# Streaming encoder step: the sampled streams' value products in one TensorE shape, with zero rows where the other half's new keys would be, and the value blocks of both halves moved next to each other

## The chip, the core and the metric

The kernel runs on one core of one Trainium2 chip. A core has TensorE (matrix products and transposes; PE in the profile, its weight loads PEld), VectorE (DVE), ScalarE (ACT), GpSimd (POOL) and SyncE (SP, which here only issues transfers). Each engine works through its own queue in order and waits on semaphores for the others. The metric is device time in microseconds of one execution. Three runs of the kernel before took 1458.16, 1460.51 and 1463.31 us; the median is 1460.51.

## The reference

One inference step of an encoder with two layers (width 1024, all in 32-bit floats), for a prompt of 512 frames and for 8 running streams of 16 new frames each (the "samples"). Layer 0 is a convolution module and a feed-forward part; then one shared set of keys and values is projected; layer 1 projects queries, attends to the shared keys, and has a feed-forward part of its own. The part that matters here is the samples' attention, per head (16 heads of 64):

```
def band_attention_sample(q, k_all, v_all, table):
    B, S, H, Dh = q.shape
    W = k_all.shape[1] - S
    bias = rel_bias_band(table, S, W + S, W)
    s = jnp.einsum("bqhd,bkhd->bhqk", q, k_all).astype(jnp.float32) * scale + bias
    p = jax.nn.softmax(s, axis=-1).astype(v_all.dtype)
    return jnp.einsum("bhqk,bkhd->bqhd", p, v_all).reshape(B, S, H * Dh)
```

Each stream's 16 queries see 512 cached keys and the 16 new ones, 528 in all. The prompt's 512 frames attend to each other in chunks of 64.

## The kernel before, in words

Frames lie along the free side, features along the 128 partitions: 640 columns, the 128 sample frames first. Large products are split into a rounded high part and a remainder and done as three products (`mm3`, lines 199 to 201; the feed-forward parts use line 439). The attention stage takes the 16 heads as 8 pairs of two heads (128 features). For a pair, a list of letters (`BO`, for the last pair `BL`, lines 67 and 68) sets the order in which the steps are written; the framework's list scheduler then orders each engine's instructions by its own timing estimate, and fills in projections of the next pair, output projections and, in the last pair, pieces of the output projection ("o" and "q" in `BL`).

The digit behind a letter is a head (a, b) or a half of the samples (s, t, n, c, d). A half is 4 streams with 16 frames and 2 heads: 4 x 32 rows = 128 partitions.

- `a` (`head_a`, line 1258 on): prompt scores of one head, bias and maximum on DVE, exponentials on ACT. `b` (`head_b`): ten transposes of them, copied out of PSUM in three pieces. `p` (`pair_c`, line 1326): the pair's value product (weights 128 rows x 64 columns), then split by ACT and DVE (lines 187 and 189).
- `s` (`samp_a`): the half's keys and values are loaded (2 x 512 KB each, line 1337, into 8 rotating buffers); four products of 512 cached keys (line 1342), one per stream, whose weights are 128 x 32 and whose outputs stand in 32 partitions each; four more for 64 columns of new keys (line 1345); the other streams' new keys get a large negative bias. DVE adds the bias and takes the maximum into a tile `Ss` (128 x 576, two rotating buffers), ACT makes the exponentials there.
- `t` (`samp_b`): the 512 cached columns are transposed in four pieces (line 1358) and copied by ACT into `PTs` (line 1368). `n` (its `rest`): the columns of the 64 new keys are transposed (line 1364) and copied by DVE (line 1365). Because the half's new values lie in rows 0 to 63 or 64 to 127 of the value tile `VT`, the transpose is 64 wide for the first half; for the second it takes 64 columns more so that the result lands in rows 64 to 127.
- `c` (`samp_c`): the half's value products, 16 over the cached keys (line 1378, weights 128 rows x 32 columns) and 4 over the new keys (line 1382, weights 64 rows x 32 columns), all into one PSUM tile. Each shows as two instructions in the profile (32 and 8 a block). DVE scales the rows into a tile `os` (line 1387).
- `d` (its `rest`): `os` is transposed (line 1391) and split into high part and remainder.

Transposes and value products go through two rotating PSUM buffers called `am`: each new user takes the one used before last, so it waits until that one has been copied out.

Of the kernel before, what the change touches and what calls it, by code (L numbers as in the profile page):

```python
# [8 lines left out]
F32 = mybir.dt.float32  # L9
F32R = mybir.dt.float32r  # L10
I32 = mybir.dt.int32
AF = mybir.ActivationFunctionType
# [3 lines left out]
P = 128  # L16
# [66 lines left out]
def tile_trunk(ctx, tc, xT, vecs, hist, w_pw1, w_pw2, w_in0, w_out0, w_os0, w_in1, w_out1, w_os1,  # L83
               w_kq, w_v, w_o, rel, kc, vc, y_out, convp_out, convs_out, k_out, v_out):
    nc = tc.nc
# [15 lines left out]
    def nm(s):  # L101
        uid[0] += 1
        return f"{s}_{uid[0]}"
# [19 lines left out]
    ident = cst.tile([P, P], F32, name="ident", tag="ident")  # L123
# [1074 lines left out]
    fill, step_end = None, [None]  # L1198
# [132 lines left out]
    def samp_a(p, u, st):  # L1331
        qb, kt = qbd[p % 2], kts[p]
        cache = []
        for src in (kc[p, u], vc[p, u].rearrange("p b k d -> p b (k d)")):
            for i in range(2):
                t = ap.tile([P, 2, 512], F32, tag="cache", name=nm("cache"), bufs=CB)
                nc.sync.dma_start(t, src[:, 2 * i:2 * i + 2, :])
                cache.append(t)
        KC, VC = cache[:2], cache[2:]
        qv = [qb[:, 4 * u + b, :, :].rearrange("p h q -> p (h q)") for b in range(4)]  # L1340
        for b in range(4):
            nc.tensor.matmul(st[32 * b:32 * b + 32, 0:512], qv[b], KC[b // 2][:, b % 2, :],
                             start=True, stop=True)
        for b in range(4):
            step_end[0] = nc.tensor.matmul(st[32 * b:32 * b + 32, 512:576], qv[b],
                                           kt[:, 64 * u:64 * u + 64], start=True, stop=True).ins
# [3 lines left out]
        addmax(S, st[:, 0:576], BS, mx[:, 0:1])  # L1350
        rs = softmax_rows(S, mx, sm, [(0, 576)])
        return S, rs, VC

    def samp_b(u, S):
        v0 = 64 * u
        tr = amt()
        for k in range(4):
            step_end[0] = nc.tensor.transpose(tr[:, k * P:(k + 1) * P],
                                              S[:, k * P:(k + 1) * P], ident).ins
        PT = ap.tile([P, 640], F32, tag="PTs", name=nm("PTs"), bufs=1)  # L1360

        def rest():
            tn = amt()
            step_end[0] = nc.tensor.transpose(tn[0:v0 + 64, 0:P], S[:, 512 - v0:576], ident).ins
            nc.vector.tensor_copy(PT[v0:v0 + 64, 512:640], tn[v0:v0 + 64, 0:P])
            return PT

        nc.scalar.activation(out=PT[:, 0:512], in_=tr, func=AF.Copy)
        return rest

    def samp_c(p, u, PT, rs, VC):
        v0 = 64 * u
        VT = vts[p // 2]
        pv = amt()
        for k in range(5):
            for b in range(4):
                if k < 4:
                    nc.tensor.matmul(pv[32 * b:32 * b + 32, 0:P],
                                     PT[:, k * P + 32 * b:k * P + 32 * b + 32],
                                     VC[b // 2][:, b % 2, k * P:(k + 1) * P], start=(k == 0), stop=False)  # L1380
                else:
                    step_end[0] = nc.tensor.matmul(
                        pv[32 * b:32 * b + 32, 0:P],
                        PT[v0:v0 + 64, 512 + 32 * b:512 + 32 * b + 32],
                        VT[v0:v0 + 64, 0, (p % 2) * P:(p % 2) * P + P], start=False, stop=True).ins
# [12 lines left out]

        return rest
# [18 lines left out]
    for p in range(NP):  # L1418
# [8 lines left out]
        for op in (BL if p == NP - 1 else BO).split():  # L1427
# [9 lines left out]
            elif op[0] == "n":  # L1437
                ps[i] = ps[i]()
            elif op[0] == "c":
                ps[i] = samp_c(p, i, ps[i], *sa[i][1:])  # L1440
            elif op[0] == "d":
                ps[i]()
            elif op[0] in "oq":
# [244 lines left out]
```

## Time and profile before

| | us |
|---|---|
| runs | 1458.16, 1460.51, 1463.31 |
| profiled execution, its span from first to last instruction | 1460.0 |
| convolution layer and first feed-forward part | 0 to about 660 |
| attention stage, first scores to last pair product | 695 to 1003 |
| second feed-forward part and final norm | 1003 to 1460 |

The execution that the profiler recorded has a span of 1460.0 us, which is the only time given for it; the median of the timed runs is 0.5 us above it. In the rows of the profile, "128*32" is the shape of the weights (rows by columns), then comes the shape of the moving side; "x32" counts merged instructions, and the time of such a row runs from the start of its first to the end of its last. "[0.20 <-issue]" is idle time of the engine ahead of the row, with what ended it; "issue" means that nothing in the profile was waited for. Since products overlap in the array, their durations are longer than the distance of their starts, and it is the starts that tell what a product costs.

### The profile page before, as it was taken

The numbers are of one execution on the slowest core, as the hardware profiler recorded it, in microseconds if no ns is written. First come the engines' busy times: TensorE is split into PE (matmuls) and PEld (weight loads), VectorE is DVE, ScalarE is ACT, GpSimd is POOL, SyncE is SP. The second block draws the span as 40 slices with busy tenths as digits, with TensorE's granted clock in tenths as the row PEclk, the third lists the DMA queues.
The fourth block names the chain that finished last, engine by engine and source line by source line (L and its number), as shares of the span: only waits on it lengthen the run. The fifth ranks groups of instructions, "written<-read, shape, count | busy, mean of one in ns | idle before, by whom it ended". The sixth has DMA issues, their size and how long they took to land. (4 is left out here: it accounts for less than half of the span.)

```text
span 1460.0 us, 28194 instructions
## 1 busy us (share of the span) xinstructions
PE 1434.0 (98%) x11022; PEld 1369.6 (94%) x11022; DVE 1138.9 (78%) x2520; ACT 757.8 (52%) x1628; POOL 297.6 (20%) x349
## 2 busy tenths in 40 slices
PE   9999999999999999999999999999999999999998
PEld 8998799999999999999987898878999999999998
DVE  6789867988888888756768668577898888888765
ACT  4666554654554554545654355443554564455453
POOL 5699120010111111013222121011011111111101
PEclk9999999999999999999999999999999999999999
DMA  7267434045444534425556554452125444444522
GB/s 243 73 180 187 126 86 146 14 135 150 131 108 118 163 92 135 116 88 193 181 163 213 173 192 162 138 200 67 44 82 143 135 113 129 137 120 109 155 66 72
DMA packets 66932, 192.56 MB, mean 132 GB/s; under 512 B 12144, under 2 KB 30320, under 8 KB 58480
## 3 DMA queue, kind: packets, MB, share of 16 engines
q1 hardware_dynamic: 52432, 160.58, 33.8%
q0 software_dynamic: 13504, 29.37, 9.9%
q8 instruction: 86, 1.41, 0.4%
q10 hardware_dynamic: 864, 0.83, 0.2%
q14 instruction: 46, 0.38, 0.1%
HBM read 179.14 MB, written 11.61 MB: 131 GB/s over the span
## 5 line engine op out<-in xcount | busy, mean ns | idle before, releaser
L439 PE MATMUL mm<-XH,whi 128*128 128x320 f32 x896 | 275.9, 310 | 2.9 <-ACT t L451 2.6
L439 PE MATMUL mm<-XH,wlo 128*128 128x320 f32 x896 | 276.1, 309 | 0.0
L439 PE MATMUL mm<-XL,whi 128*128 128x320 f32 x896 | 274.5, 309 | 0.0
L371 ACT ACTIVATE whi<-raw 128x512 fp32r<-128x512 f32 (+2 forms) x280 | 168.4, 613 | 135.2 <-PE mm L439 103.6
L199 PE MATMUL mm<-xh,whi 128*128 128x320 f32 (+2 forms) x640 | 200.2, 314 | 0.8 <-DVE h L702 0.4
L200 PE MATMUL mm<-xh,wlo 128*128 128x320 f32 (+2 forms) x640 | 198.2, 311 | 0.0
L372 DVE TENSOR_TENSOR wlo<-raw,whi 128x512 fp32r<-128x512 f32 (+2 forms) x280 | 183.9, 666 | 15.9 <-ACT whi L371 14.8
L201 PE MATMUL mm<-xl,whi 128*128 128x320 f32 (+2 forms) x640 | 195.9, 311 | 0.4 <-DVE xl L189 0.4
L439 PE MATMUL mm<-hid,whi 128*128 128x320 f32 x732 | 172.5, 311 | 5.5 <-DVE hid L372 3.1
L439 PEld LDWEIGHTS mm<-XH,whi 128*128 128x128 f32 x896 | 167.7, 188 | 4.9 <-ACT t L451 4.2
L439 PEld LDWEIGHTS mm<-XH,wlo 128*128 128x128 f32 x896 | 168.2, 188 | 0.0
L439 PEld LDWEIGHTS mm<-XL,whi 128*128 128x128 f32 x896 | 167.7, 188 | 0.0
L439 PEld LDWEIGHTS mm<-hid,whi 128*128 128x128 f32 x732 | 125.0, 188 | 8.8 <-DVE hid L372 4.2
L199 PEld LDWEIGHTS mm<-xh,whi 128*128 128x128 f32 x640 | 120.5, 188 | 4.0 <-ACT xh L187 1.5
L201 PEld LDWEIGHTS mm<-xl,whi 128*128 128x128 f32 x640 | 119.7, 188 | 1.2 <-DVE xl L189 0.8
L200 PEld LDWEIGHTS mm<-xh,wlo 128*128 128x128 f32 x640 | 120.5, 189 | 0.2
L439 PE MATMUL mm<-hid,wlo 128*128 128x320 f32 x366 | 113.0, 309 | 0.0
L439 PE MATMUL mm<-XH,slo 128*128 128x320 f32 x344 | 106.0, 308 | 0.0
L439 PE MATMUL mm<-XH,shi 128*128 128x320 f32 x344 | 105.8, 309 | 0.0
L439 PE MATMUL mm<-XL,shi 128*128 128x320 f32 x344 | 105.6, 308 | 0.0
L417 POOL DMA_DIRECT2D s<-in_w_in x38 | 22.1, 581 | 388.7 <-DVE wlo L372 151.8
L841 POOL TENSOR_TENSOR ca<-ca,cvt 128x512 f32<-128x512 f32 x60 | 91.9, 1532 | 17.8 <-ACT cvt L838 11.2
(275 smaller groups left out, 3370.8 us busy)
## 6 DMA issues: line engine op xcount, KB each, us to landing
raw<-in_w_in SPq DMA_DIRECT2D x38, 1024.0 KB
s<-in_w_in POOLq DMA_DIRECT2D x76, 256.0 KB, 4.2
raw<-in_w_os SPq DMA_DIRECT2D x24, 768.0 KB
cache<-in_ck SPq DMA_DIRECT2D x32, 512.0 KB
cache<-in_cv SPq DMA_DIRECT2D x32, 512.0 KB
raw<-in_w_pw SPq DMA_DIRECT2D x11, 1024.0 KB
s<-in_w_os POOLq DMA_DIRECT2D x48, 192.0 KB, 3.6
raw<-in_w_kq SPq DMA_DIRECT2D x8, 1024.0 KB
```

Of the source, the lines that this page charges most:

```text
L199: nc.tensor.matmul(ps, wh, xh, start=(first and i == 0), stop=False)
L200: nc.tensor.matmul(ps, wl, xh, start=False, stop=False)
L201: end = nc.tensor.matmul(ps, wh, xl, start=False, stop=(stop and i == last))
L371: put_end[1] = nc.scalar.activation(out=hi, in_=src, func=AF.Copy).ins
L372: put_end[0] = nc.vector.tensor_tensor(out=lo, in0=src, in1=hi.bitcast(F32), op=sub).ins
L417: nc.gpsimd.dma_start(s1, src[:, 2 * n:3 * n])
L439: last = nc.tensor.matmul(pt, wt, v, start=(first and k == i == 0), stop=(k == n - 1 and i == 2), skip_group_check=True)
L841: nc.gpsimd.tensor_tensor(out=acc, in0=acc, in1=pr, op=ALU.add)
```

## The change

Four things change, all in the attention stage.

1. The four products over the new keys take 128 rows of weights as the others do. The probabilities of the other half's 64 rows are zero: for the first half the transpose takes 128 columns, the last 64 of which are zeros (a score tile `Sn` of 640 columns, filled with zeros there once), and the copy `PM` takes all 128 rows; for the second half a tile `PN`, with rows 0 to 63 set to zero once, takes rows 64 to 127.
2. `Ss` has one buffer (second half), `Sn` is the first half's. `PTs` is 512 wide with two buffers.
3. The row-scaled output goes into the first 128 columns of the score tile in place of `os`.
4. The order of the steps: both halves are transposed before the pair's product, and `c0 c1` and `d0 d1` are neighbours (in the last pair, all ahead of `p0`).

```diff
-BO = "a0 s0 a1 s1 b0 b1 t0 n0 p0 c0 d0 t1 n1 c1 d1"
-BL = "a0 o2 s0 a1 o2 s1 q2 t0 q2 n0 b0 q2 b1 q2 c0 q2 d0 t1 q2 n1 o2 c1 o2 d1 p0 o2"
+BO = "a0 s0 a1 s1 b0 b1 t0 n0 t1 n1 p0 c0 c1 d0 d1"
+BL = "a0 o2 s0 a1 o2 s1 q2 t0 q2 n0 b0 q2 t1 q2 b1 n1 q2 c0 c1 q2 d0 o2 d1 o2 p0 o2"
...
+    Sn = ap.tile([P, 640], F32, name="Sn", tag="Sn")
+    nc.gpsimd.memset(Sn[:, 576:640], 0.0)
+    PN = ap.tile([P, P], F32, name="PN", tag="PN")
+    nc.gpsimd.memset(PN[0:64, :], 0.0)
...
-        S = ap.tile([P, 576], F32, tag="Ss", name=nm("Ss"), bufs=2)
+        S = ap.tile([P, 576], F32, tag="Ss", name=nm("Ss"), bufs=1) if u else Sn
...
-        PT = ap.tile([P, 640], F32, tag="PTs", name=nm("PTs"), bufs=1)
+        PT = ap.tile([P, 512], F32, tag="PTs", name=nm("PTs"), bufs=2)
...
-            step_end[0] = nc.tensor.transpose(tn[0:v0 + 64, 0:P], S[:, 512 - v0:576], ident).ins
-            nc.vector.tensor_copy(PT[v0:v0 + 64, 512:640], tn[v0:v0 + 64, 0:P])
-            return PT
+            step_end[0] = nc.tensor.transpose(tn[:, 0:P], S[:, 512 - v0:640 - v0], ident).ins
+            pn = PN if u else ap.tile([P, P], F32, tag="PM", name=nm("PM"), bufs=1)
+            nc.vector.tensor_copy(pn[v0:, :], tn[v0:, 0:P])
+            return PT, pn
...
-                if k < 4:
-                    nc.tensor.matmul(pv[32 * b:32 * b + 32, 0:P],
-                                     PT[:, k * P + 32 * b:k * P + 32 * b + 32],
-                                     VC[b // 2][:, b % 2, k * P:(k + 1) * P], start=(k == 0), stop=False)
-                else:
-                    step_end[0] = nc.tensor.matmul(
-                        pv[32 * b:32 * b + 32, 0:P],
-                        PT[v0:v0 + 64, 512 + 32 * b:512 + 32 * b + 32],
-                        VT[v0:v0 + 64, 0, (p % 2) * P:(p % 2) * P + P], start=False, stop=True).ins
-        os_ = ap.tile([P, P], F32, tag="os", name=nm("os"), bufs=1)
+                c = slice(k * P + 32 * b, k * P + 32 * b + 32)
+                step_end[0] = nc.tensor.matmul(
+                    pv[32 * b:32 * b + 32, 0:P], PT[:, c] if k < 4 else pn[:, 32 * b:32 * b + 32],
+                    VC[b // 2][:, b % 2, k * P:(k + 1) * P] if k < 4
+                    else VT[:, 0, (p % 2) * P:(p % 2) * P + P], start=k == 0, stop=k == 4).ins
+        os_ = S[:, 0:P]
```

The scheduler makes a new order of it on every engine, from the first pair's transposes to the first products of the second feed-forward part. Three places on TensorE follow. Lines of the changed kernel are shifted: 1309 is 1313 now, 1326 is 1330, 1358 is 1362, 1364 is 1368, and 1378 and 1382 are both 1384. The shape behind the names is that of the output.

TensorE, seventh pair, the end of the first half's value block, before (cache: the values; vt: the new ones; KK, KL, QQ: the next pair's split scores):

```order
L1378 MATMUL am_11256<-cache_11117,PTs_11240 32x128 x2
L1378 MATMUL am_11256<-cache_11119,PTs_11240 32x128 x2
L1382 MATMUL am_11256<-vt_10921,PTs_11240 32x128 x4
L1285 MATMUL w_1351_11494<-KK_11496,QQ_11498 128x512
L1286 MATMUL w_1351_11494<-KL_11497,QQ_11498 128x512
```

The same place in the changed kernel:

```order
L1384 MATMUL am_11258<-cache_11109,PTs_11231 32x128 x2
L1384 MATMUL am_11258<-cache_11111,PTs_11231 32x128 x2
L1384 MATMUL am_11258<-vt_10913,PM_11235 32x128 x4
L1384 MATMUL am_11280<-cache_11171,PTs_11242 32x128 x2
L1384 MATMUL am_11280<-cache_11173,PTs_11242 32x128 x2
```

The new keys' products are of the line and shape of the others, and the second half's block follows at once. This is so in the fifth, seventh and eighth pairs; in the first four and the sixth other products stand between the two blocks.

TensorE, seventh pair, the transposes ahead of the pair's product, before (S: prompt probabilities; Ss: a half's; PT with vt: the pair's product):

```order
L201 MATMUL mm_11442<-xl_7448,whi_11325 128x384
L1309 MATMUL am_11231<-ident,S_11138 128x128 x2
L1358 MATMUL am_11235<-ident,Ss_11129 128x128 x4
L1364 MATMUL am_11242<-ident,Ss_11129 64x128
L1326 MATMUL am_11245<-PT_11201,vt_10921 64x512
```

and now:

```order
L201 MATMUL mm_11432<-xl_7448,whi_11315 128x384
L1313 MATMUL am_11216<-ident,S_11129 128x128 x4
L1313 MATMUL am_11222<-ident,S_11129 128x128 x2
L1362 MATMUL am_11226<-ident,Sn 128x128 x4
L1368 MATMUL am_11233<-ident,Sn 128x128
L1362 MATMUL am_11237<-ident,Ss_11183 128x128 x4
L1368 MATMUL am_11244<-ident,Ss_11183 128x128
L1330 MATMUL am_11247<-PT_11192,vt_10913 64x512
```

Six users of the two `am` buffers stand in a row ahead of the pair's product, where there were three; in the fifth pair, too, the second half's transposes stand right ahead of it.

TensorE, eighth pair, the first half's remainder and the first head's transposes, before:

```order
L1364 MATMUL am_11678<-ident,Ss_11567 64x128
L1309 MATMUL am_11682<-ident,S_11491 128x128 x4
L1309 MATMUL am_11688<-ident,S_11491 128x128 x4
L1309 MATMUL am_11694<-ident,S_11491 128x128 x2
L199 MATMUL mm_11698<-ohi_9955,whi_11530 128x320
```

and now:

```order
L1368 MATMUL am_11667<-ident,Sn 128x128
L199 MATMUL mm_11659<-ohi_9951,whi_11520 128x320
L200 MATMUL mm_11659<-ohi_9951,wlo_11521 128x320
L201 MATMUL mm_11659<-olo_9952,whi_11520 128x320
L199 MATMUL mm_11659<-ohi_10499,whi_11520 128x320
L200 MATMUL mm_11659<-ohi_10499,wlo_11521 128x320
L201 MATMUL mm_11659<-olo_10500,whi_11520 128x320
L1313 MATMUL am_11672<-ident,S_11481 128x128 x4
L1313 MATMUL am_11678<-ident,S_11481 128x128 x4
```

Six products of the output projection stand between them now.

More of the change, by code (lines that the diff above doesn't have):

```diff
@@ L1359, in samp_b, with samp_c @@
                                               S[:, k * P:(k + 1) * P], ident).ins
-        PT = ap.tile([P, 640], F32, tag="PTs", name=nm("PTs"), bufs=1)
+        PT = ap.tile([P, 512], F32, tag="PTs", name=nm("PTs"), bufs=2)
         def rest():
             tn = amt()
-            step_end[0] = nc.tensor.transpose(tn[0:v0 + 64, 0:P], S[:, 512 - v0:576], ident).ins
-            nc.vector.tensor_copy(PT[v0:v0 + 64, 512:640], tn[v0:v0 + 64, 0:P])
-            return PT
-        nc.scalar.activation(out=PT[:, 0:512], in_=tr, func=AF.Copy)
+            step_end[0] = nc.tensor.transpose(tn[:, 0:P], S[:, 512 - v0:640 - v0], ident).ins
+            pn = PN if u else ap.tile([P, P], F32, tag="PM", name=nm("PM"), bufs=1)
+            nc.vector.tensor_copy(pn[v0:, :], tn[v0:, 0:P])
+            return PT, pn
+        nc.scalar.activation(out=PT, in_=tr, func=AF.Copy)
         return rest
-    def samp_c(p, u, PT, rs, VC):
+    def samp_c(p, u, PTs, S, rs, VC):
         v0 = 64 * u
+        PT, pn = PTs
         VT = vts[p // 2]
@@ L1439, in tile_trunk @@
             elif op[0] == "c":
-                ps[i] = samp_c(p, i, ps[i], *sa[i][1:])
+                ps[i] = samp_c(p, i, ps[i], *sa[i])
             elif op[0] == "d":
```

2 lines of the change are left out of this document (1 added, 1 removed).

## The prediction

> **What bounds the kernel now.** I read the page first (shares by engine, then the chain that ended last), then the busy time of the attention stage alone, then TensorE's rows around one value block.
>
> ```profile
> span 1460.0 us, 28194 instructions
> PE 1434.0 (98%) x11022; PEld 1369.6 (94%) x11022; DVE 1138.9 (78%) x2520; ACT 757.8 (52%) x1628; POOL 297.6 (20%) x349
> PEclk9999999999999999999999999999999999999999
> PE 27%; DVE 2%; DMA 1%; ACT 0%; issue 0%; DVEq 0%
> ```
>
> TensorE is busy for 98% of the span at full clock, and it is the only engine with a real share of the chain. The attention stage, where all of the change lies, is no exception:
>
> ```profile
> 695.00:1003.00 308.00, 303.25 (x2742) 263.23 (x2742) 212.53 (x636) 150.77 (x404) 55.79 (x93) 1.00 0.51 169
> 960.00:1003.00 43.00, 40.18 (x402) 31.32 (x401) 29.24 (x82) 16.95 (x42) 4.61 (x9) 1.00 0.25 89
> ```
>
> The columns are length, then PE, PEld, DVE, ACT and POOL busy. PE is busy for 303 of 308 us, DVE for 213, so a microsecond taken from TensorE's own sequence here is a microsecond of the span, unless a wait takes its place. More than half of the idle time (2.8 of 4.8 us) lies in the last 43 us, where projections no longer fill the gaps. A busy PE still hides something: each product is booked for 0.27 us or more while the next starts 0.03 to 0.23 us later, so short gaps do not show as idle. They show in the starts, and in the weight loads' idle time:
>
> ```profile
> 730.26 0.81 PEld L1378 LDWEIGHTS am<-cache,PTs 128*32 128x32 f32 x32 [0.17 <-issue]
> 730.26 1.08 PE L1378 MATMUL am<-cache,PTs 128*32 128x128 f32 x32
> 731.27 0.15 PEld L1382 LDWEIGHTS am<-vt,PTs 64*32 64x32 f32 x8 [0.20 <-issue]
> 731.27 0.42 PE L1382 MATMUL am<-vt,PTs 64*32 64x128 f32 x8
> 731.62 0.19 PEld L1285 LDWEIGHTS w<-KK,QQ 128*128 128x128 f32 x1 [0.20 <-issue]
> PEld am L1382 <- issue: 3.0, 15, 0.2
> ```
>
> "128*32" is the weights' shape, rows by columns. The last row is from the waits of the stage: the first weight load of the 64*32 products stood idle for 0.2 us in 15 of 16 blocks, with nothing that the profile names to wait for, 3.0 us in all. The same pause stands wherever the shape changes, and not where it stays.
>
> **The change, term by term.**
>
> *The pause before the new keys' products (removed).* 32 products from 730.26 take 1.08 us, the last one itself 0.27, so they start every (1.08 - 0.27)/31 = 0.026 us and the last starts at 731.07. The 64*32 products start at 731.27: 0.20 after it, in place of 0.026. With all products in 128*32 the step is an ordinary one: 16 blocks x 0.174 = -2.8 us.
>
> *The products themselves (dearer).* Eight 64*32 products take (0.42 - 0.28)/7 = 0.020 us each, eight in 128*32 would take 0.026: 7 x 0.006 x 16 = +0.7 us. The weight loads say the same: 8 in 0.15 us there, 32 in 0.81 here.
>
> *Shape changes next to the blocks.* Over the whole order of the eight pairs I count the points where neighbouring products differ in shape (transposes counted as full ones): 91 before, 69 after. Of the 22 that go, 16 are those above. Four are "64*32, then the sampled scores", which also are 128*32:
>
> ```profile
> 743.06 0.42 PE L1382 MATMUL am<-vt,PTs 64*32 64x128 f32 x8
> 743.41 1.06 PE L1342 MATMUL w<-cache,qbd 128*32 128x512 f32 x8
> 744.30 0.29 PE L1345 MATMUL w<-kt,qbd 128*32 128x64 f32 x8
> 744.52 0.45 PE L199 MATMUL mm<-xh,whi 128*128 128x384 f32 x1
> ```
>
> Last start 743.06 + 0.42 - 0.28 = 743.20, next 743.41: 0.21 where 0.026 would do, so 4 x 0.19 = -0.8. The other two are one entry and one exit (the halves' blocks touch in only three of eight pairs, the fifth, seventh and eighth; elsewhere the scheduler still puts 12 to 26 projection products, or scores, between). An exit from 128*32 is 744.52 - (744.30 + 0.29 - 0.22) = 0.15 after a 64-column product, of which about 0.03 is the step; an entry:
>
> ```profile
> 741.78 0.34 PE L201 MATMUL mm<-xl,whi 128*128 128x384 f32 x1
> 742.05 1.08 PE L1378 MATMUL am<-cache,PTs 128*32 128x128 f32 x32
> 777.24 0.33 PE L200 MATMUL mm<-xh,wlo 128*128 128x384 f32 x1
> 777.41 0.34 PE L201 MATMUL mm<-xl,whi 128*128 128x384 f32 x1
> ```
>
> 0.27 in place of 0.17, so 0.10. Together -0.2. The exit after a 128-column 128*32 product has no row; the nearest are 0.15 above and 0.21 after 64*32, and I take it to be like the latter, so no term.
>
> *The remainder's transpose.* For the first half it loads 128 columns in place of 64:
>
> ```profile
> 724.24 0.28 PE L199 MATMUL mm<-xh,whi 128*128 128x256 f32 x1
> 724.37 0.27 PE L1364 MATMUL am<-ident,Ss 128*64 128x128 f32 x1
> 724.39 0.36 PE L200 MATMUL mm<-xh,wlo 128*128 128x256 f32 x1
> 724.60 0.28 PE L201 MATMUL mm<-xl,whi 128*128 128x256 f32 x1
> 776.83 0.28 PE L201 MATMUL mm<-xl,whi 128*128 128x256 f32 x1
> 776.95 0.27 PE L1364 MATMUL am<-ident,Ss 128*128 128x128 f32 x1
> 776.98 0.42 PE L199 MATMUL mm<-xh,whi 128*128 128x384 f32 x1
> 777.24 0.33 PE L200 MATMUL mm<-xh,wlo 128*128 128x384 f32 x1
> ```
>
> Narrow: 0.13 before it and 0.02 + 0.21 behind it. Wide: 0.12, then 0.03 + 0.26 with a moving side of 384 in place of 256 columns, which accounts for the 0.05. Nothing for the width: 0, at most +0.05 x 8 = +0.4. The narrow transpose shows no pause. The Trainium skill says that changing the tiling mode, not just the tile, drains TensorE (page "TensorEngine Tiling", section Key Properties); the trace agrees for products (0.20 us), not for this transpose. By that rule eight narrow transposes would each cost two pauses, and the sum below would be lower by 8 x 2 x 0.17 = 2.7 us.
>
> *The rest.* Two more fills on POOL come once, before the first pair, while POOL is idle 80% of the time. The copy of the remainder has 128 lanes in place of 64 for one half, on DVE, busy 213 of 308 us; the row-scaled output now lies in the score tile, which is thus held until its last transpose, and the DVE maximum that refills it in the next pair queues behind that. Cover for both is the projection products; without it the wait is at most the ~0.7 us of score products that stand between. No term; bounds 0 and +0.7 x 8.
>
> *Waits that move.* The two work buffers in PSUM ("am") turn over in order: whoever takes one waits for the copy of its use before last. The seventh pair:
>
> ```profile
> 964.68 0.60 PE L1358 MATMUL am<-ident,Ss 128*128 128x128 f32 x4
> 965.14 0.41 DVE L1315 COPY PT<-am 128x256 f32<-128x256 f32 x1
> 965.61 0.30 PE L1364 MATMUL am<-ident,Ss 128*64 128x128 f32 x1 [0.32 <-DVE PT L1315]
> 965.94 0.28 DVE L1365 COPY PTs<-am 64x128 f32<-64x128 f32 x1 [0.39 <-PE am L1364]
> 966.28 1.94 PE L1326 MATMUL am<-PT,vt 128*64 128x512 f32 x10 [0.38 <-DVE PTs L1365]
> ```
>
> Four transposes start at 964.68, the next should be 0.44 later but is at 965.61 (0.49 lost), the pair's product at 966.28 in place of 965.72 (0.56 lost). In the new order both halves' transposes stand there without a product between them. A copy of 512 columns holds a buffer 0.25 + 0.6 us after the last transpose, so the second four lose some 0.75, the product another 0.75, the first ones 0.8 together: 2.3 in place of 1.05, +1.3. The fifth pair has one such place more, +0.8. The eighth gains:
>
> ```profile
> 974.84 0.33 PE L1364 MATMUL am<-ident,Ss 128*128 128x128 f32 x1
> 975.89 0.47 PE L1285 MATMUL w<-KK,QQ 128*128 128x512 f32 x1 [0.73 <-DVE QQ L1277]
> 985.54 0.66 PE L1309 MATMUL am<-ident,S 128*128 128x128 f32 x4 [0.59 <-DVE PTs L1365]
> ```
>
> Here 0.9 is lost waiting for the split keys, and 0.8 at 985.54 where a remainder's transpose stands right ahead of others. In the new order the value blocks and two sets of score products stand ahead of the first, six projection products ahead of the second: about -1.5 of the 1.7. In the third pair a chain of copies without cover goes as well:
>
> ```profile
> 795.70 0.66 PE L1358 MATMUL am<-ident,Ss 128*128 128x128 f32 x4 [0.39 <-ACT PT L1313]
> ```
>
> 0.55 at this row, and about as much at the transposes ahead of it: -1.1. Sum of the moved waits: +1.3 + 0.8 - 1.5 - 1.1 = -0.5, with bounds of -3 (most of the stage's 4.8 us idle goes) and +5 (0.6 us lost in each of eight pairs).
>
> *Sum.* -2.8 + 0.7 - 0.8 - 0.2 - 0.5 = -3.6 us against the profiled span of 1460.0: 1456.4. The median of the timed runs, 1460.51, lies 0.5 above that span, so the forecast is **1456.9 us**, -0.25%.
>
> **The rivals.**
>
> *The moved waits go nearly all.* Pauses -3.1, waits -3 and the scattered ones too: about -7, 1453.5. For it: no pair now lacks cover except the fifth and seventh. Against: every engine's order is new from the first pair on, and new neighbours bring new waits.
>
> *The narrow transposes pay, as in the rule above:* -3.6 - 2.7 = -6.3, 1454.2. The rows at 724.37 speak against it.
>
> *Slower: the second half's value block waits for the pair's split.* With the blocks together, its buffer is the one of the pair's product, to be split by ACT and DVE first; before, another block and a transpose lay between:
>
> ```profile
> 730.38 0.60 ACT L187 ACTIVATE ohi<-am 128x512 fp32r<-128x512 f32 x1 [5.58 <-PE am L1326]
> 731.01 0.69 DVE L189 TENSOR_TENSOR olo<-am,ohi 128x512 fp32r<-128x512 f32 x1 [6.05 <-ACT ohi L187]
> 966.61 2.29 DVE L180 TENSOR_TENSOR wlo<-raw,whi 128x2048 fp32r<-128x2048 f32 x1 [0.38 <-ACT whi L175]
> ```
>
> The buffer is free at 731.7; a block straight behind the first half's would start at 731.3. That is 0.4 us a pair, and up to 1 if DVE is at something long (2.29 us in one row). From 0.45 us in each of eight pairs it eats the gain; at 1 us it gives -3.6 + 8 = +4.4: 1464.9. Against it: the order puts 2 us or more of products between the pair's product and that block everywhere.
>
> *Nothing gained: it is not what it says.* Blocks touch in three pairs only; if the pauses go and the waits return as much, 1460.5.
>
> **How the numbers follow.** Forecast (1455 to 1459.5) 0.50; waits gone 0.17; transposes pay 0.10; slower 0.15; nothing 0.08. What a measurement of this kernel can tell from no change is about 0.3%, 4.4 us, so faster means below 1456.1. That takes the two fast rivals nearly whole (0.26) and a fifth of the forecast (0.10): 0.36. Slower is beyond 1464.9, which is the upper half of the slow rival and a little of the unknown bounds: 0.10. The rest, 0.54, is no change. The range cuts half of each outer case: 1453.0 to 1461.0; the forecast's own is 1455 to 1459.5.
>
> **What would show it.** Right: no 64*32 rows; the value products in steps of 0.026 throughout, the waits row of that load's issue gone, 22 pauses fewer; PE's busy time in the stage less by about 3 us; the stage's idle time again near 5 us, with more of it in the seventh pair and less in the eighth. Wrong: value blocks preceded by waits for the pair's split (ACT "ohi" or DVE "olo"), a transpose step that shrinks in the first half, or an idle sum of the stage that differs by more than 3 us.

## The result: 4 us slower

The changed kernel takes 1464.04 us (median of 21 runs, 1461.32 to 1467.70), the kernel before on the same chips 1460.02 us (21 runs): a ratio of 1.0027, with a 95% interval of 1.0021 to 1.0033. The forecast was 1456.9 with a range of 1453.0 to 1461.0; size and sign are both wrong.

### The profile page after: what moved, and what is told of

Its sections match the earlier page's. It is cut to its first block, busy times and chain, and to the rows that moved or that the text cites. A ratio compares the mean times of both kernels' runs of the same rounds, so it can differ in the third digit from the quotient of the medians.

```text
span 1461.5 us, 28195 instructions
## 1 busy us (share of the span) xinstructions
PE 1431.6 (98%) x11022; PEld 1369.4 (94%) x11022; DVE 1141.6 (78%) x2520; ACT 756.9 (52%) x1628; POOL 300.2 (21%) x351
```

## The profile after

First the page of the changed kernel (shares, clock, chain), then the busy time of the stage and of its last 43 us, in the windows used before.

```profile
span 1461.5 us, 28195 instructions
PE 1431.6 (98%) x11022; PEld 1369.4 (94%) x11022; DVE 1141.6 (78%) x2520; ACT 756.9 (52%) x1628; POOL 300.2 (21%) x351
PEclk9999999999999999999999999999999999999999
PE 25%; DVE 2%; DMA 2%; ACT 0%; issue 0%; DVEq 0%; ACTq 0%
695.00:1003.00 308.00, 300.39 (x2728) 262.28 (x2728) 211.92 (x633) 150.38 (x404) 61.01 (x96) 1.00 0.52 171
960.00:1003.00 43.00, 39.27 (x403) 31.58 (x403) 31.11 (x89) 18.02 (x45) 5.95 (x11) 1.00 0.44 128
```

In the first window TensorE's busy time falls by 2.9 us (303.25 to 300.39) and its idle time rises by the same 2.9 (4.8 to 7.6). The window is 308 us long for both kernels, so the two must mirror each other, and the fall says nothing of the removed pauses. The **stage** itself tells them apart. I take it from the first pair's first scores to the last "ohi, wlo" product over the last pair's outputs; before and changed kernel, its two ends and the busy time between them:

```profile
694.83 0.39 PE L1285 MATMUL w<-KK,QQ 128*128 128x512 f32 x1
1020.52 0.31 PE L200 MATMUL am<-ohi,wlo 128*128 128x320 f32 x1
694.83:1020.52 325.69, 320.58 (x2860) 280.02 (x2859) 228.76 (x669) 159.31 (x421) 59.86 (x97) 1.00 0.50 165
692.59 0.40 PE L1289 MATMUL w<-KK,QQ 128*128 128x512 f32 x1
1021.11 0.31 PE L200 MATMUL am<-ohi,wlo 128*128 128x320 f32 x1
692.59:1021.11 328.52, 319.67 (x2860) 280.94 (x2859) 229.49 (x669) 159.28 (x421) 63.03 (x97) 1.00 0.50 164
```

The stage takes 325.69 us before and 328.52 after: +2.8. Busy falls by 0.9, idle rises by 3.7 (5.1 to 8.85). What was removed did go; the value products show it. Three rows around a first half's block and five around two neighbouring blocks, changed kernel:

```profile
806.53 1.08 PE L1384 MATMUL am<-cache,PTs 128*32 128x128 f32 x32
807.43 0.40 PE L1384 MATMUL am<-vt,PM 128*32 128x128 f32 x8
807.76 0.44 PE L199 MATMUL mm<-ohi,whi 128*128 128x384 f32 x1
888.31 1.08 PE L1384 MATMUL am<-cache,PTs 128*32 128x128 f32 x32
889.21 0.40 PE L1384 MATMUL am<-vt,PM 128*32 128x128 f32 x8
889.42 1.06 PE L1384 MATMUL am<-cache,PTs 128*32 128x128 f32 x32
890.30 0.40 PE L1384 MATMUL am<-vt,PN 128*32 128x128 f32 x8
890.63 0.39 PE L200 MATMUL mm<-ohi,wlo 128*128 128x256 f32 x1
```

A block now occupies 806.53 to 807.76, 1.23 us; before it was 742.05 to 743.41, 1.36 us. 16 blocks x 0.13 = 2.1 us, as much as the two first terms of the sum together (-2.8 + 0.7). The row of 64*32 weight loads that waited for "issue" in 15 places is gone. New, or longer than before, are these waits of the weight loads, whole stage:

```profile
PEld mm L199 <- DVE h L1259: 4.2, 10, 0.7
PEld am L1313 <- ACT PT L1317: 2.1, 4, 0.8
PEld w L1289 <- DVE mx L1198: 1.8, 1, 1.8
```

The output projection's products stand for DVE's additions that free their PSUM buffer: 4.2 us in 10 places, where the kernel before had 0.7 us in 3. The prompt transposes' wait for ACT's copies was 1.0 us in 2 places before. One set of prompt scores, the eighth pair's, stands 1.8 us for DVE's maximum.

The rest of these two profiled executions (2.2 less ahead of the stage, 0.9 more behind) is of the size by which all kernels below differ there without regard to the edit: the stage starts between 690.6 and 697.3 us and is followed by 437.9 to 440.4 us. So I compare kernels by the stage, and by the timed runs for the verdict. Of the 4.0 us between the medians the stage shows 2.8; where the other 1.2 lie is not shown. The stage is from one profile of each kernel. How well it repeats can be seen in three kernels below that have the same order in pairs one to seven and the first half's tile freed: their eighth pair's first prompt scores start 272.7, 272.8 and 272.9 us after the stage's start.

## The experiments

All are the changed kernel or the kernel before with a few lines edited; the diffs are against the kernel that the sentence names. The times stand together here, with 11 runs of each experiment but for "order and held tile" (5) and "output projection moved" (4). The ratio is to the kernel before on the same chip (medians there 1459.27 to 1460.29 us); it is not the quotient of the two medians and can lie up to 0.1% from it. The stage is from one profile each.

| run | median us | ratio (95%) | stage us |
|---|---|---|---|
| kernel before | 1460.02 | 1 | 325.69 |
| changed kernel | 1464.04 | 1.0027 (1.0021 to 1.0033) | 328.52 |
| shape alone | 1457.95 | 0.9982 (0.9973 to 0.9991) | 323.45 |
| changed, old order | 1459.14 | 0.9990 (0.9981 to 0.9999) | 323.57 |
| order alone | 1460.23 | 1.0001 (0.9992 to 1.0010) | 326.73 |
| changed, tile freed | 1459.92 | 1.0004 (0.9995 to 1.0013) | 324.09 |
| order and held tile | 1464.36 | 1.0032 (1.0019 to 1.0044) | 330.89 |
| only first half freed | 1458.91 | 0.9998 (0.9989 to 1.0007) | 324.10 |
| only second half freed | 1462.76 | 1.0021 (1.0012 to 1.0029) | 329.21 |
| old order, pairs 1 to 7 | 1457.84 | 0.9987 (0.9978 to 0.9996) | 324.05 |
| late d0, held | 1458.34 | 0.9996 (0.9987 to 1.0005) | 324.96 |
| early d0, held | 1459.30 | 1.0003 (0.9994 to 1.0012) | 327.15, part of it at half clock |
| freed, old order 1 to 7 | 1457.60 | 0.9988 (0.9980 to 0.9997) | 323.31 |
| freed, old order last | 1457.51 | 0.9988 (0.9980 to 0.9997) | 323.90 |
| late d0, freed | 1457.38 | 0.9990 (0.9980 to 0.9999) | 324.32 |
| d0 ahead of pair product | 1461.17 | 1.0022 (1.0012 to 1.0032) | 331.25, part of it at half clock |
| output projection moved | 1474.69 | 1.0101 (1.0088 to 1.0114) | 341.02, part of it at half clock |
| held, old order, old shape | 1460.18 | 1.0006 (0.9998 to 1.0015) | 325.30 |

Three of these stages hold stretches in which the profile shows TensorE's granted clock at half; in all the others the clock is full throughout. Here are the stretches of "early d0, held" (first row) and of "d0 ahead of pair product" (the clock is the third number from the end):

```profile
984.50:987.90 3.40, 3.40 (x17) 3.36 (x16) 1.51 (x3) 0.00 (x0) 1.80 (x2) 0.50 0.35 61
791.30:798.10 6.80, 6.43 (x27) 5.42 (x30) 6.62 (x23) 3.21 (x9) 1.55 (x3) 0.50 0.05 11
989.20:992.60 3.40, 3.36 (x16) 2.92 (x15) 1.55 (x3) 0.59 (x1) 1.77 (x2) 0.51 0.50 111
```

In the second of them products with 256 columns start every 0.21 us, where 0.12 is usual. If TensorE lost half of each stretch, which is the most, the stages at full clock would be 325.4 (early d0) and 326.1 (d0 ahead); the moved output projection has two stretches of 3.4 us and would be at 337.6. These are estimates; a stage at full clock should lie between them and the table's. The timed runs of these three kernels have a lower mean clock, too (0.9974, 0.9965 and 0.9962, with 0.9985 or 0.9986 for the kernel before on the same chips; the others are within 0.0009 of it). A clock lower by 0.001 is at most 1.5 us of 1460, so their times hold up to 1.6, 3.1 and 3.5 us of it. Ahead of each of these five stretches TensorE is busy for only 1.1 to 2.4 of 4 us, which may have to do with it, and then the lost time would be a price of the waits that these kernels make. But the changed kernel with the old order has 1.8 of 4 us in one place (980.5 to 984.5) and stays at full clock, so that is not shown.

### Which of the three parts costs: shape, order or held tile

The change consists of three things that can be taken apart: the products' shape, the order of the steps, and the sampled outputs that now lie in the score tile and so hold it.

**Shape alone** (changed kernel, with the order, `BL` included, and the tiles of before):

```diff
-BO = "a0 s0 a1 s1 b0 b1 t0 n0 t1 n1 p0 c0 c1 d0 d1"
+BO = "a0 s0 a1 s1 b0 b1 t0 n0 p0 c0 d0 t1 n1 c1 d1"
...
-        PT = ap.tile([P, 512], F32, tag="PTs", name=nm("PTs"), bufs=2)
+        PT = ap.tile([P, 512], F32, tag="PTs", name=nm("PTs"), bufs=1)
-        os_ = S[:, 0:P]
+        os_ = ap.tile([P, P], F32, tag="os", name=nm("os"), bufs=1)
```

> The new keys' products in the 128-row shape with the zero rows, as in the change; the order of steps, the output tile of the sampled half and the single transposed-weights tile as before the change. Profiled spans: 1460.0 us before, 1461.5 after the change. Theory A (the pauses are worth what was summed for them, and the order of steps costs the rest): about 2.1 to 2.9 us under the kernel before, 1457 to 1458, since all value blocks lose 0.13 us and nothing else moves. Theory B (the held score tile costs the rest): the same, 1457 to 1458, since this kernel does not hold it. Theory C (the shape itself costs, through the longer vector copies of the zero rows or the wider transposes): 1460 or more.

Measured: 0.18% faster, stage -2.24 us. As A and B said; C falls.

**Changed kernel with the old order** (`BO` and `BL` of before, nothing else):

> The changed kernel with the order of steps from before, so that the two value blocks stand apart again; the score tile still holds the sampled outputs until their transpose. Theory A (order costs): 1457 to 1458.5, nearly the same as the shape alone. Theory B (the held score tile costs): 1460 or more, 3 us or so above the shape alone. Theory C (the shape costs): 1460 or more, and the same as the shape alone.

Stage 323.57, time 1459.14: against the shape alone the held tile costs 0.1 us in the stage here, and 1.2 in the medians, whose intervals overlap. By the stage as A said, by the time between A and B.

**Order alone** (kernel before with the new `BO` and `BL`, `PTs` with two buffers):

> The kernel before with the new order of steps and nothing else of the change, but a second buffer for the transposed weights, which the order needs: the 64-row products and their pauses are there, the score tile is freed early. Theory A (the order costs about 6 us): 1465 to 1467, above both kernels. Theory B (the held score tile costs): 1459 to 1461. Theory C (the shape costs): 1459 to 1461, the kernel before within its noise.

Time as before, stage +1.04. Theory A falls: the order by itself costs nothing like 6 us.

**Score tile freed early** (changed kernel):

```diff
-        os_ = S[:, 0:P]
+        os_ = PT[:, 0:P]
```

> The changed kernel, with the sampled outputs written over the transposed weights, which are dead by then, and not over the scores: the next pair's addition to the score tile no longer waits for the last transpose of this pair. Theory A (order costs): 0 to 2 us under the changed kernel, 1462 to 1464, the 1.8 us wait of the eighth pair's scores gone and the rest as it was. Theory B (the held score tile costs): 1458 to 1460. Theory C (the shape costs): 1462 to 1464.

One line brings the stage from 328.52 to 324.09, -4.4 us, and the time from 1.0027 to 1.0004 of the kernel before, as B said here. So the cost needs both, the new order and the held tile: A falls by the order alone, and B, in the stage, by the old order with the tile held. The projection's wait, 4.2 us in the changed kernel, is less; the eighth pair's waits for a maximum are not gone, but stand now 0.5 us at its prompt scores and 1.1 at its sampled ones:

```profile
PEld mm L199 <- DVE h L1259: 1.9, 4, 0.5
PEld w L1346 <- DVE mx L1198: 1.1, 1, 1.1
PEld w L1289 <- DVE mx L1198: 0.5, 1, 0.5
```

### Does it need the new shape, and which half's tile is it

**Order and held tile with the old products** (the order-alone kernel, in which the outputs go over the scores):

```diff
-        os_ = ap.tile([P, P], F32, tag="os", name=nm("os"), bufs=1)
+        os_ = S[:, 0:P]
```

> The order alone, of the earlier run, and one thing more: the sampled outputs go over the scores, as in the change, so that the score tile is held until their transpose. The 64-row products stay. So far, in the attention stage (first scores of the first pair to the last products over its outputs): before 325.7 us, changed kernel 328.5, order alone 326.7, changed kernel with the tile freed 324.1, changed kernel with the old order 323.6. Theory D (the held tile costs 4 us, and only in the new order, whatever the shape): stage 330.5 to 331.5, time 1464 to 1465.5. Theory E (the cost needs the new shape as well, by its wider copies): stage 326.5 to 328, time 1460 to 1461.5.

Stage +4.16 over the order alone, 1464.36 us: D, and the shape has no part in it.

**Only one half's tile freed** (changed kernel; the mirror has the two names exchanged):

```diff
-        os_ = S[:, 0:P]
+        os_ = S[:, 0:P] if u else PT[:, 0:P]
```

> The changed kernel with only the first half's score tile freed early; the second half's is still held until its transpose. Theory D1 (the first half's tile is what costs: the eighth pair's scores stood 1.8 us behind its refill): stage 324 to 325.5, time 1460 to 1461. Theory D2 (the second half's tile costs, since its transpose is the last step of a pair): stage 327.5 to 328.5, time 1463 to 1464. If each holds some: between.

> The mirror of the run before: only the second half's score tile is freed early. Theory D1 (the first half's tile costs): stage 327.5 to 328.5, time 1463 to 1464. Theory D2 (the second half's): stage 324 to 325.5, time 1460 to 1461.

324.10 and 329.21: the first is in D1's range, the second 0.7 us above it (the times are 1.1 and 0.2 us below what D1 said). All of the cost is the first half's tile.

**New order in the last pair only**:

> The changed kernel with the old order of steps in pairs one to seven and the new one in the last pair alone. The waits that I ascribe to the held tile (output projection behind the vector engine's additions in the third and fifth pairs, 4.2 us; the eighth pair's scores, 1.8 us) come from the order of pairs one to seven: by that, stage 323 to 324.5 and time 1458 to 1459.5, as with the old order throughout. If the last pair's order is the loser: stage 327 to 328.5, time 1462 to 1464.

324.05, within what was expected: the loss sits in pairs one to seven.

### What a held tile does in the new order

The traces of the changed kernel and of the one with the first half freed show it best in the third pair. TensorE in the changed kernel, the third pair's first-half sampled scores and second head's prompt scores, then the previous pair's last transpose of `Sn`:

```profile
762.28 0.28 PE L1349 MATMUL w<-kt,qbd 128*32 128x64 f32 x4
762.49 0.50 PE L1289 MATMUL w<-KK,QQ 128*128 128x512 f32 x1
778.83 0.33 PE L1393 MATMUL am<-ident,Sn 128*128 128x128 f32 x1
785.32 1.07 PE L1346 MATMUL w<-cache,qbd 128*32 128x512 f32 x8
```

And DVE in the same kernel:

```profile
767.70 0.42 DVE L1215 TENSOR_TENSOR kt<-mm,bc 128x256 f32<-128x256 f32 x1 [1.82 <-DMA cache<-in_ck]
...
770.67 0.42 DVE L1215 TENSOR_TENSOR qt<-mm,bc 128x256 f32<-128x256 f32 x1 [1.98 <-PE mm L201]
773.61 0.69 DVE L189 TENSOR_TENSOR olo<-am,ohi 128x512 fp32r<-128x512 f32 x1 [2.52 <-ACT ohi L187]
774.24 0.35 DVE L1389 TENSOR_SCALAR Sn<-am,rs 128x128 f32<-128x128 f32 x1
778.96 0.35 DVE L1389 TENSOR_SCALAR Ss<-am,rs 128x128 f32<-128x128 f32 x1 [4.38 <-PE am L1384]
779.30 0.76 DVE L1198 CUSTOM_DVE_ANT_0 Sn<-w,BS 128x576 f32<-128x576 f32 x1
779.99 0.08 DVE L1198 DVE_READ_ACCUMULATOR2_ANT mx<- 128x1 f32 x1
779.99 0.69 DVE L1198 CUSTOM_DVE_ANT_0 S<-w,BP 128x512 f32<-128x512 f32 x1
```

With the first half's tile freed (its stage starts 1.15 us later by the profile's clock), DVE does the same two things here:

```profile
763.22 0.76 DVE L1198 CUSTOM_DVE_ANT_0 Sn<-w,BS 128x576 f32<-128x576 f32 x1 [1.79 <-PE w L1349]
...
766.28 0.68 DVE L1198 CUSTOM_DVE_ANT_0 S<-w,BP 128x512 f32<-128x512 f32 x1
```

The sampled scores are in PSUM at about 762.6 in the changed kernel. They are read at 779.30, right behind the transpose at 778.83 that frees `Sn`; freed, the same row comes at 763.22, as soon as the products are there. DVE takes its queue in order, and the prompt scores of the second head (products from 762.49) stand behind that row: read at 779.99 against 766.28. Meanwhile DVE is idle for 1.8 + 2.0 + 2.5 + 4.4 = 10.7 us in the rows shown. The refill itself shows no wait: the list scheduler has put it behind the row at 778.96, which waits for the second half's block. A held tile therefore acts through the order that the scheduler makes of it as well as through the waiting; no run here takes the two apart. The scores' PSUM is not handed back either, so the second half's scores come at 785.32 in place of 772.28. Then all of the softmax work and the copies of two halves and two heads fall into one stretch, in which DVE has no gap over 0.8 us until 803, and there the projection's additions come late, as in the first of these TensorE rows (third pair, changed kernel); in the second, of the eighth pair, prompt scores wait for the maximum of the refill:

```profile
801.15 0.39 PE L199 MATMUL mm<-ohi,whi 128*128 128x256 f32 x1 [0.44 <-DVE h L1259]
980.10 0.39 PE L1289 MATMUL w<-KK,QQ 128*128 128x256 f32 x1 [1.65 <-DVE mx L1198]
```

Over the stage, TensorE is idle for 8.85 us in the changed kernel and for 6.8 in the one with the first half freed:

```profile
693.74:1017.84 324.10, 317.29 (x2861) 281.07 (x2860) 229.54 (x669) 158.92 (x421) 56.92 (x97) 1.00 0.50 166
```

So 2.0 of the 4.4 us show as idle time; the other 2.4 lie in busy time, 319.67 against 317.29 us for the same products, that is in starts that come later while earlier products are still booked.

### How much of it is the time of release

**Old order with d0 moved to the end, held**: `BO = "a0 s0 a1 s1 b0 b1 t0 n0 p0 c0 t1 n1 c1 d0 d1"` and the old `BL` in the changed kernel.

> The changed kernel with the old order of steps and one step moved in pairs one to seven: the first half's last transpose (d0), which frees its score tile, from right behind its value block to the end of the pair, ahead of the second half's. The value blocks stay apart. With the old order untouched the stage took 323.6 us and the time was 1459.1. Theory D (the score tile of the first half is refilled for the next pair only after that transpose, and the vector engine works in order, so a late transpose pushes the next pair's whole score work back): 3 to 5 us more, stage 326.5 to 328.5, time 1462 to 1464. Theory F (it is the adjacent blocks and their buffers that cost together with the held tile): stage 323 to 324.5, time 1458.5 to 1460.

Stage 324.96, +1.4 over the old order untouched; time 1458.34. Less than D said (3 to 5 more), a little more than F's in the stage and none in the time.

**New order with d0 between the blocks, held**: `c0 d0 c1 d1`.

> The changed kernel with one step moved: d0 stands between the two value blocks (c0 d0 c1 d1), so that the held score tile is freed by a block and its neighbours earlier; the pair's first-half refill can then start some 3 us earlier (in the third pair 776 in place of 779.3 us). Theory D: part of the 4.4 us comes back, 1 to 3.5: stage 325 to 327.5, time 1460.5 to 1463. Theory F: nothing comes back while both transposes stand ahead of the pair's product, stage 328 to 329, time 1463.5 to 1464.5.

1.0027 becomes 1.0003 and the stage 327.15, with up to 1.7 us of that at half clock, so part of the cost comes back, as D said; F falls. The half clock comes late: the eighth pair's second prompt scores start 280.4 us after the stage's start, against 284.4 in the changed kernel and 279.6 with the first half freed, so that up to there 4.0 of 4.8 us are won back. The refill waits openly for the transpose here:

```profile
775.21 0.76 DVE L1198 CUSTOM_DVE_ANT_0 Sn<-w,BS 128x576 f32<-128x576 f32 x1 [0.49 <-PE am L1393]
```

**Late d0 with the first half freed**:

> The old order with d0 moved to the end of the pair, as in the earlier run (stage 325.0 us, 1.4 above the old order untouched), but with the first half's score tile freed early. Theory D (the 1.4 us is the late refill of the held tile): stage 323.3 to 324, as the shape alone. Theory H (it is the moved step's other effects, as its place among the two work buffers): stage 324.7 to 325.3.

324.32, between the two. Of the 1.4 us some 0.6 is the holding, 0.8 the order.

**First half's block and d0 ahead of the pair's product**: `t0 n0 t1 n1 c0 d0 p0 c1 d1` in the changed kernel.

> The changed kernel with the first half's value block and last transpose ahead of the pair's product (c0 d0 p0 c1 d1): the held tile is freed some 3 to 5 us earlier than with c0 d0 behind it (stage 327.2 us), some 7 earlier than in the changed kernel (328.5). Theory D (the cost follows the time of release): stage 324.5 to 326, third pair's refill 78 to 80 us after the stage's start, where the changed kernel has 86.7. Theory I (the new order's cost comes whenever both halves' transposes stand ahead, and the release hardly matters): 327 or more.

Stage 331.25 as it was profiled, which looks like I and a miss for D. But up to 5.1 us of it are the half clock, more than in any other stage here; at full clock it would be 326.1 at the least, 0.1 above D's range and below I's. So this run decides nothing between D and I. The refill comes 81.9 us after the stage's start (4.8 earlier than in the changed kernel, not 7 to 9), and other waits take over, for ACT's copies of transposes:

```profile
PEld am L1313 <- ACT PT L1317: 3.2, 4, 2.0
PEld am L1368 <- ACT PTs L1373: 2.2, 3, 1.4
```

**Output projections one pair earlier**: `PO = {1: 0, 3: 1}`.

> The changed kernel with the two output projections that stand in the third and fifth pairs written one pair earlier, in the second and fourth; the held tile and the order stay. In the changed kernel most of the new waits stand beside those projections. Theory J (a late refill is cheap by itself, and dear only where the projections' additions crowd the vector engine as well): the waits do not follow the projections, stage 325 to 327. Theory D (the late refill crowds the vector engine in every pair, and whatever fills TensorE there waits for it): the waits move with the projections, stage 327.5 to 329.5.

341.02, outside both theories also without its 3.4 us of half clock: in the window from 695 to 1020 TensorE is idle for 18 of 325 us. The move takes cover from the later pairs, which costs more than what it was to show. It tells nothing on J or D.

**Held tile alone in the kernel before**:

> The kernel before with one change: the sampled outputs go over the scores, so that the score tile is held until their transpose; old order, 64-row products. With the new shape this step cost 0.1 us in the stage in the old order. If that is so for the old shape too: stage 325.5 to 326.5 (before 325.7), time within 1 us of the kernel before. If the new shape hid a cost of it: 327 or more.

325.30, 0.2 below the range of the first case, and the time is 0.9 us above that of the kernel before: in the old order the held tile is free in the stage with the old shape too.

The runs that differ by the holding of the first half's tile, in order of what it does to the third pair's refill (us after the stage's start):

| order, shape | refill free | refill held | stage, held less free |
|---|---|---|---|
| old, new shape | 76.9 | 79.7 | +0.1 |
| old, old shape | 77.0 | 80.0 | -0.4 |
| old with late d0, new shape | 69.8 | 82.9 | +0.6 |
| new, new shape | 69.5 | 86.7 | +4.4 |
| new, old shape | 69.9 | 87.4 | +4.2 |

In the old order the refill comes late anyway, since d0 comes early and the next pair's scores late, so holding moves it by 3 us only. In the new order it would come early, and the holding moves it by 17. The cost rises with the shift, but not in proportion: 13 us cost 0.6 in the old order. In the new order d0 between the blocks puts the refill at 82.4, also 13 us late, and its stage is 1.3 to 3.1 us above the kernel with the first half freed, the lower figure with the half clock taken out. By this the last 4 us of the shift cost at least 1.4 of the 4.4. Why they are so dear, and how much the order adds at an equal shift, is not settled.

### A version that beats both

**Freed tile with mixed orders**, two runs (the freed-tile kernel with the old `BO`, and with the old `BL`):

> A candidate: score tile freed early (outputs over the transposed weights), the old order in pairs one to seven, the new one in the last pair. If the three effects add (shape -2.3, last pair's order between -0.5 and +0.5, no held tile): stage 323 to 324, time 1457.5 to 1458.5, as the shape alone (323.5, 1458.0).

> The other mix: score tile freed early, the new order in pairs one to seven and the old one in the last. The new order cost 0.6 to 1.0 us in the stage without the held tile. If that lies in the last pair: stage 323 to 323.5, time 1457.5 to 1458. If it lies in pairs one to seven: stage 324 to 324.5, time 1459 to 1460, as with the tile freed (324.1, 1459.9).

Stages 323.31 and 323.90, both 0.12% faster than before. The first is the shape alone again; the second, between its two expectations, by its stage puts the order's 0.6 us rather into pairs one to seven and by its time rather into the last, which can't be told apart at this size. The shape alone has the lowest ratio, 0.9982, and is faster than the kernel before and than the changed one; between it, these two and the others near 0.999 the runs don't decide.

## Why the prediction was wrong, point by point

**The pauses and the dearer products (-2.8 + 0.7): the sum right, both terms wrong, and so by luck.** A block lost 0.13 us, 2.1 in 16 blocks. But the forecast took the mean step of a block, 0.026 us, for its ordinary step. This is the view of the block at 806.53 up to 806.66:

```profile
806.53 0.32 PE L1384 MATMUL am<-cache,PTs 128*32 128x128 f32 x4
```

Four products have started, the last at 806.53 + 0.32 - 0.30 = 806.55 (they are booked for 0.30 us here, for 0.27 later), and no fifth follows up to 806.66. The 32 products are eight such groups: the last one starts at 806.53 + 1.08 - 0.27 = 807.34, so it is (807.34 - 806.55)/7 = 0.11 us from group to group, 0.02 in a group and 0.09 between two. The pause ahead of the new keys' products stands between two groups. It was 0.20 and became 0.09 (807.34 to 807.43): 16 x 0.11 = -1.8, not -2.8. And the eight products of the new keys did not become dearer: (0.40 - 0.27)/7 = 0.019 us each, against 0.020 before, so the rest of the 2.1, about -0.3, stands in place of +0.7. The stage loses 2.24 us by the shape in the old order (323.45 against 325.69), 2.64 in the new with the tile freed (324.09 against 326.73), 2.37 with it held (328.52 against 330.89). The exit after the 128-column products, for which there was no row, was taken as 0.21: the last of the products at 807.43 starts at 807.43 + 0.40 - 0.27 = 807.56 and the next product at 807.76, 0.20.

**"64*32, then sampled scores" (-0.8): right in kind, too large.** Where such a place remains, in the kernel with the first half freed,

```profile
772.07 0.40 PE L1384 MATMUL am<-vt,PM 128*32 128x128 f32 x8
772.28 1.04 PE L1346 MATMUL w<-cache,qbd 128*32 128x512 f32 x8
```

the step is 772.28 - (772.07 + 0.40 - 0.27) = 0.08, the step between groups again and not 0.026: 4 x (0.21 - 0.08) = 0.5. With this the shape alone should have given 2.1 + 0.5 = 2.6; it gave 2.2.

**The remainder's transpose (0): right.** The shape alone widens all eight narrow transposes. With the 2.7 us that the rival asked for them, its stage would be 5.3 shorter; it is 2.2. The Trainium skill says in "TensorEngine Tiling (Array Packing)", section Key Properties, that a change of tiling mode drains TensorE; here the measurement agrees for the 64*32 products (0.20 us between starts in place of 0.09) and not for a transpose that loads 64 columns.

**Waits that move (-0.5): wrong sign.** With the tile freed or never held, the new order costs +0.6 (shape new) or +1.0 (old) in the stage, though it also saves entries and exits. The seventh pair was sized well: 2.3 was forecast, and the changed kernel loses, by the starts, 0.5 + 0.5 + 0.4 + 0.4 = 1.8 at its transposes and the pair's product. The gains were not there: the eighth pair lost its wait for split keys, but got those for the maximum (with the tile freed still 0.5 and 1.1 us), and the third pair's copies without cover came back as waits for the additions.

**The held score tile ("No term; bounds 0 and +0.7 x 8"): this is the step that failed.** It measured +4.4, inside the bound, and I left it out of the sum. The sentence named the right wait ("the DVE maximum that refills it in the next pair queues behind that"), and priced it by what TensorE would lose at the score products, at most 0.7 us a pair. Most of it is not paid there: in the open, score products stand for a maximum 1.8 us in the eighth pair, more than double the price, and 0.7 in the fourth. What queues behind the refill on DVE is a pair's whole softmax work, and the order's other half, d0 moved from behind its block to the end of the pair, put the release late. I costed the order and the tile apart; in the stage each alone is nearly free (+0.6 to +1.0, and -0.4 to +0.1), and together they cost some 4 more than the order alone. How the late refill turns into this sum is shown in part only, as said above.

The terms as measured: -2.4 for the shape (mean of the three), +0.8 for the order, +4.4 for the tile, +2.8 in all. The stage has +2.8, and must: each term is a difference of stages along the way from one kernel to the other, so the agreement proves nothing further. By the ratios the same three steps are -0.18%, +0.22% and +0.23%, each sure to about 0.1% either way. The timed runs thus bear out the shape and the tile, and leave the order's share open: with the old shape it is +0.01% by them.

**The rivals.** The one on the slower side ended on the right side by the wrong mechanism: no value block waits for the pair's split. In the waits of the changed kernel these weight loads have 1.5 us of "issue" and 0.2 us each for three other tiles, none of them `ohi` or `olo`. "Waits go nearly all" and "transposes pay" are both refuted by the stage's idle time and the shape alone. "Nothing gained" (chance 0.08) was the nearest in kind: the pauses went and waits came back, but twice as much as had gone. The test named in the prediction, an idle sum that differs by more than 3 us, comes out at 2.9 in the window of the forecast and at 3.7 over the stage: a window whose ends do not move with the work hid it. The busy time "less by about 3 us", named as a sign of being right, was met in that window for the same reason, and is 0.9 over the stage.

## What to carry to other kernels

When a buffer's last reader is moved later, ask what refills it and list everything that stands behind that refill in its engine's queue: the price can be that whole tail, and not the one product that waits. Cost a reordering and a change of what holds a buffer together, because one decides when the other's release comes. Test a bundled change part by part: here one part gave 0.18%, and two that were nearly free alone in the stage took it back twice. Compare busy time over the same work, not over the same microseconds, and look at the granted clock of a stretch before its length is put down to an edit. And before a mean step is used as a price, see whether the products come evenly.

## What the runs showed of the hardware that was not expected

128*32 products do not start evenly every 0.026 us: four start within 0.02 us, and the next group 0.09 us later. The same 0.08 to 0.09 stands at the change to new values and at the change to 512 columns, as long as the weights stay 128*32, against 0.20 where they change to 64*32. In three of the profiled executions TensorE ran at a granted clock of 0.50 for stretches of 3.4 or 6.8 us in the stage. And a kernel whose TensorE is 98% busy was not limited by the sum of its products: DVE, busy 212 of 308 us in the window, stood idle for over 10 us in one stretch, while finished scores waited 17 us in PSUM behind rows of its queue, and in the stretch after that TensorE waited for it.
